# Rotary embedding and attention scores: three of the k loads issued by GpSimd over 15 of the 16 DMA engines

## The chip, the core and the metric

The kernel runs on one core of a Trainium2 chip. TensorE (PE) multiplies matrices into PSUM, VectorE (DVE) and ScalarE (ACT) work on tiles and copy out of PSUM, GpSimd (POOL) and SyncE (SP) issue transfers, and sixteen DMA engines move data between the large memory (DRAM) and the on-chip memory (SBUF). The engines run on their own and wait for each other through semaphores. The metric is the time of one execution in microseconds (us) on the device.

## What is computed

Queries `q` and keys `k` have the shape batch 16, sequence 512, heads 16, dimension 64, all float32. Both are rotated by position (the two halves of the 64 values are mixed by `cos` and `sin`), and then each head's queries are multiplied with all keys of the same batch and head:

```python
q1, q2 = q[..., :half_dim], q[..., half_dim:]
cos_q = cos[None, :, None, :]
sin_q = sin[None, :, None, :]
q_rot = np.concatenate([q1 * cos_q - q2 * sin_q, q1 * sin_q + q2 * cos_q], axis=-1)
...
scores = np.einsum('bshd,bthd->bsht', q_rot, k_rot)
return scores.astype(np.float32)
```

The output has 16 x 512 x 16 x 512 values, 268 MB; the two inputs together are 67 MB.

## The kernel before

**Tiling.** A batch's 512 positions are laid over 128 partitions with four positions (C = 4) in each, so a load of q or k for one batch is one transfer of 128 rows of 16 KB, 2048 KB, and it is contiguous in DRAM. There are 64 steps `i` (16 batches x 4 position classes). In a step the scores of 128 positions with all 512 keys are made for 16 heads: eight pairs `p`, each with two matmuls into one of three PSUM tiles `ps` (L364), which ACT copies into a staging tile `st` (L373). When the eighth pair is copied, SP stores the whole staging tile, 128 rows of 32 KB, 4096 KB (L381). There are three staging tiles, so step i + 3 can only be copied into a tile when the store of step i has landed. The first batch is arranged differently: its inputs arrive in four smaller loads (`load_units`), and its four steps are stored in 16 transfers of 1024 KB.

**Rotation and transposes.** DVE rotates q and k in place in the input tiles, with three operations per position class (`rope`, L290). PE transposes the rotated tile in blocks of 128 (L315), and DVE (for q) or ACT (for k) copies the result from PSUM into `qT` or `kT` (L333). The rotation runs one to two steps ahead for q and about a batch ahead for k: in step i the classes i + 2 of q and i + 5 of k are rotated, and the classes i + 1 of q and i + 4 of k are transposed.

**Loads.** q and k have two input tiles each (`q_sb0`, `q_sb1`, `k_sb0`, `k_sb1`), taken in turn by batch. `load(which, b)` adds one transfer to SP's queue. At the end of step i with i % 4 == 3 the load of k for batch i // 4 + 3 is added (L465), at i % 4 == 2 that of q for batch i // 4 + 2 (L463). So SP's queue is: store, store, load q, store, load k and so on, in this order. SP issues a store when ACT has made the last copy into its tile; a load of k follows at once, since its tile was free by then.

**Order and semaphores.** Every operation is written into a `Plan` with an engine, the keys that it reads and the keys that it writes. `resolve` (L38) derives each operation's waits: a reader waits for the last writer of a key, a writer for the last writer and all readers since. A wait that is implied by another one is dropped. An operation's event is its engine's count, or, for a transfer, 16 more on a semaphore of its own. `emit` writes the operations of SP, ACT, POOL and DVE in order with their waits, and PE's steps as a loop of eight steps per turn. The keys of an input tile are `("in", which, b % 2, c)`, one for each position class; `src_key` (L261) gives the key that the rotation and the transposes use.

POOL has no part in the steady work: it builds the identity matrix for the transposes at the start and is then idle.

Of the kernel before, what the change touches and what calls it, by code (L numbers as in the profile page):

```python
# [7 lines left out]
PE, ACT, DVE, POOL, SP = "PE", "ACT", "DVE", "POOL", "SP"  # L8
# [11 lines left out]
class Plan:  # L20
# [17 lines left out]
    def resolve(self):  # L38
        writer, readers, also = {}, {}, {}
        count = {}  # L40
        known = {e: {} for e in (PE, ACT, DVE, POOL, SP)}
        clock = {}

        def merge(a, b):
            for s, v in b.items():
                a[s] = max(a.get(s, 0), v)

        for op in self.ops:
            need = {}
            for k in op.reads:  # L50
                if k in writer:
                    merge(need, dict([writer[k]]))
            for k in op.writes:
                if k in writer:
                    merge(need, dict([writer[k]]))
                for s, v in readers.get(k, {}).items():
                    merge(need, {s: v})
                if k in also and op.sem is None:
                    merge(need, also.pop(k))
            kn = known[op.engine]  # L60
            need = {s: v for s, v in need.items() if kn.get(s, 0) < v}
            if op.engine == PE:
                need.pop(PE, None)
            for s in list(need):
                others = [t for t in need if t != s]
                if any(clock[t, need[t]].get(s, 0) >= need[s] for t in others):
                    del need[s]
            op.waits = need
            for s, v in need.items():
                merge(kn, clock[s, v])  # L70
                merge(kn, {s: v})
            if op.sem is None:
                s, v = op.engine, count.get(op.engine, 0) + 1
            else:
                s, v = op.sem, count.get(op.sem, 0) + 16
            count[s] = v
            op.event = (s, v)
            clock[s, v] = dict(kn)
            clock[s, v][s] = v
            if op.sem is None and op.engine != PE:  # L80
                clock[s, v][op.engine] = v
            for k in op.reads:
                readers.setdefault(k, {})
                merge(readers[k], {s: v})
            for k in op.writes:
                writer[k] = (s, v)
                readers[k] = {}
            for k in op.also:
                also.setdefault(k, {})
                merge(also[k], {s: v})  # L90
        self.count = count
        self.seen = known

    def emit(self, handles, first, period, turns):

        nc = self.nc
        eng = {PE: nc.tensor, ACT: nc.scalar, DVE: nc.vector, POOL: nc.gpsimd, SP: nc.sync}

        def plain(op):  # L100
            waits = list(op.waits.items())
            for s, v in waits[1:]:
                eng[op.engine].wait_ge(handles[s], v)  # L103
            a, b = op.emit()
            for s, v in waits[:1]:
                a.wait_op(handles[s], v, "sem-ge")
            s, _ = op.event
            b.then_inc(handles[s], 1 if op.sem is None else 16)

        for e in (SP, ACT, POOL, DVE):  # L110
            for op in self.ops:
                if op.engine == e:
                    plain(op)
        for s, v in self.count.items():
            if s not in (PE, ACT, DVE, POOL) and self.seen[SP].get(s, 0) < v:
                nc.sync.wait_ge(handles[s], v)

        pe = [op for op in self.ops if op.engine == PE]
        last = first + period * turns
        for op in pe:  # L120
            if op.step < first:
                plain(op)
        body = [[op for op in pe if (op.step - first) // period == j] for j in range(turns)]
        up = {}
        for s in (ACT, DVE):
            seen = []
            for j in range(2):
                seen.append(sum(1 for op in self.ops if op.engine == s and op.sem is None and op.step < first + period * j))
            up[s] = seen[1] - seen[0]
        n = len(body[0])  # L130
        assert all(len(b) == n for b in body)
        waits = []
        for m in range(n):
            w = {}
            for j in range(turns):
                for s, v in body[j][m].waits.items():
                    w[s] = max(w.get(s, 0), v - j * up[s])
            waits.append(w)
        low, regs, now = {}, {}, {}
        for s in (ACT, DVE):  # L140
            vs = []
            for w in waits:
                if s in w:
                    vs.append(w[s])
            assert vs == sorted(vs) and vs[0] > 0, vs
            low[s] = vs[0]
            regs[s] = nc.tensor.alloc_register("wait_" + s)
            nc.tensor.reg_mov(regs[s], vs[0])
            now[s] = vs[0]
        add = mybir.AluOpType.add  # L150
        with nc.Fori(0, turns, engines=[mybir.EngineType.PE], hint_back_edge=False):
            for m, op in enumerate(body[0]):
                ws = list(waits[m].items())
                for s, v in ws:
                    if v != now[s]:
                        nc.tensor.reg_alu(regs[s], regs[s], v - now[s], add)
                        now[s] = v
                for s, v in ws[1:]:
                    nc.tensor.wait_ge(handles[s], nc.tensor.snap(regs[s]))
                a, b = op.emit()  # L160
                for s, v in ws[:1]:
                    a.wait_op(handles[s], regs[s], "sem-ge")
                b.then_inc(handles[PE], 1)
            for s in (ACT, DVE):
                nc.tensor.reg_alu(regs[s], regs[s], low[s] + up[s] - now[s], add)
        for op in pe:
            if op.step >= last:
                plain(op)
# [3 lines left out]
def kernel(  # L172
# [8 lines left out]
    nc = tc.nc  # L181
    fp32 = mybir.dt.float32
    mult = mybir.AluOpType.mult
    add = mybir.AluOpType.add

    B, S, H, D = q.shape
    HD = D // 2
    P = 128
    C = S // P
# [6 lines left out]
    pool = ctx.enter_context(tc.tile_pool(name="sb", bufs=1))  # L196
    psum = ctx.enter_context(tc.psum_pool(name="ps", bufs=1))

    dram = {
        "q": q.rearrange("b (p c) h d -> b p c h d", c=C),  # L200
        "k": k.rearrange("b (p c) h d -> b p c h d", c=C),
    }
    o_v = out.rearrange("b (p c) h t -> b c p h t", c=C)

    ident = pool.tile([P, P], fp32, name="ident")
    cos_t = pool.tile([P, C, HD], fp32, name="cos_t")
    sin_t = pool.tile([P, C, HD], fp32, name="sin_t")
    ss_t = pool.tile([P, C, 2, HD], fp32, name="ss_t")
    part = pool.tile([P, H * D], fp32, name="part")
    stage = [pool.tile([P, H, S], fp32, name=f"st{n}") for n in range(NST_BUFS)]  # L210
    inb = {w: [pool.tile([P, C, H * D], fp32, name=f"{w}_sb{n}") for n in range(2)] for w in "qk"}
    kTb = [pool.tile([P, HP, S], fp32, name=f"kT{n}") for n in range(2)]
# [6 lines left out]
    plan = Plan(nc)  # L219
# [8 lines left out]
    def dma(engine, e, dst, src, sem, reads=(), writes=(), also=()):  # L228
        plan.add(engine, one(lambda: e.dma_start(dst, src)), reads, writes, sem=sem, also=also)
# [9 lines left out]
    def load_units(which, head, heads):  # L239
# [9 lines left out]
            writes=[("unit", which, u) for u in us], also=[x for u in us for x in unit_keys(which, u)],  # L249
        )  # L250

    def load(which, b):
        if b >= B:
            return
        t = inb[which][b % 2]
        dma(
            SP, nc.sync, t.rearrange("p c (h d) -> p c h d", h=H), dram[which][b], f"in_{which}{b % 2}",
            writes=[("in", which, b % 2, c) for c in range(C)],
        )

    def src_key(which, n):  # L261
        return ("unit", which, n) if n < C else ("in", which, n // C % 2, n % C)

    def src_also(which, n):
        return unit_keys(which, n) if n < C else ()

    def rope(which, n):
# [16 lines left out]
            swapped = bass.AP(part.tensor, part.offset + HD, [part.ap[0], (D, H), (-HD, 2), (1, HD)])  # L284
            adds = [(x4, swapped)]
        xs, xc = x.rearrange(sv, **k2), x.rearrange(sv, **k1)
        key, more = src_key(which, n), src_also(which, n)

        def tt(o, a, b, op, reads, writes):
            plan.add(DVE, one(lambda: nc.vector.tensor_tensor(o, a, b, op=op)), reads, writes, also=more)  # L290

        def products():
            tt(pv, xs, ss, mult, [key, "ss"], ["part"])
            tt(xc, xc, cs, mult, [key, "cos"], [key])

        def sums():
            for y, z in adds:
                tt(y, y, z, add, [key, "part"], [key])

        return [products, sums]  # L300

# [2 lines left out]
    def transposed(which, n, g, engine):  # L304
# [10 lines left out]
            done = [nc.tensor.transpose(bank[:, x, :], srcs[x], ident) for x in range(4)]  # L315
            return done[0], done[-1]

        plan.add(PE, emit, [src_key(which, n), "ident"], [("bank", m)], also=src_also(which, n))
        src = bank
        if which == "q":  # L320
            dst = qTb[n % 2][:, 4 * g : 4 * g + 4, :]
# [180 lines left out]
```

## Time and profile before

| | us |
|---|---|
| median of 3 runs (803.38 to 803.93) | 803.67 |
| the profiled execution | 804.24 |
| its span, first to last instruction | 802.5 |

What the transfers look like, from the list of DMA issues (size and median time from issue to landing):

| transfer | count | KB each | us to landing |
|---|---|---|---|
| store of a staging tile | 60 | 4096 | 24.7 |
| load of k | 15 | 2048 | 27.7 |
| load of q | 15 | 2048 | 28.7 |
| store of a quarter, first batch | 16 | 1024 | 12.3 |

The time to landing includes the wait behind the transfers that were issued earlier. In all, 67.24 MB are read and 268.44 MB written, 418 GB/s over the span. SP waits 722.3 us in total for ACT's copies, which is its normal state: it issues a store when the tile is full. A reader should take the DMA share as the mean over the sixteen engines: a share of 0.06 can be one engine that works while fifteen stand still.

### The profile page before, as it was taken

What the parts mean: (1) busy time and instruction counts of PE and PEld (TensorE: products, weight loads), DVE (VectorE), ACT (ScalarE), POOL (GpSimd) and SP (SyncE); (2) the same over time, 40 slices, a digit from 0 to 9 for tenths busy, and PEclk for the clock granted to TensorE, in tenths of its full rate; (3) what the DMA queues carried; (4) which work ended last, traced back from release to release, by engine and by line L of the source; (5) the groups of instructions that cost most, each with busy time, mean ns of one, the idle gap of its engine ahead of it and who ended that gap; (6) DMA issues with size and microseconds to landing.
All of it is one profiled execution on the core that took longest, in us unless ns stands there. A gap on an engine that the chain in (4) does not pass through costs nothing.

```text
span 802.5 us, 8182 instructions
## 1 busy us (share of the span) xinstructions
PE 688.5 (86%) x3072; PEld 298.0 (37%) x3072; DVE 545.2 (68%) x516; ACT 562.5 (70%) x647; POOL 0.7 (0%) x6
## 2 busy tenths in 40 slices
PE   3989998998979989698896988979879899789970
PEld 2444443333424334243342433434333344334430
DVE  6999987666767668576585866848758477585400
ACT  2978886866858668586676866768757687678770
POOL 0000000000000000000000000000000000000000
PEclk9999999998999989999899999989989799899995
DMA  9999999999999999999999999999999999998994
GB/s 347 419 425 435 432 414 426 427 433 433 426 430 432 427 439 417 441 425 439 428 430 434 431 432 426 437 430 423 426 428 407 433 412 420 429 434 358 419 439 199
DMA packets 17681, 335.87 MB, mean 419 GB/s; under 512 B 1792, under 2 KB 3072, under 8 KB 4096
## 3 DMA queue, kind: packets, MB, share of 16 engines
q1 hardware_dynamic: 17376, 335.55, 98.3%
q10 hardware_dynamic: 288, 0.13, 0.1%
q8 instruction: 6, 0.10, 0.0%
q14 instruction: 11, 0.09, 0.0%
HBM read 67.24 MB, written 268.44 MB: 418 GB/s over the span
## 4 chain that ended last, share of the span: by engine, by line
DMA 48%; PE 38%; DVE 6%; ACT 5%; issue 0%; ACTq 0%; DVEq 0%; SPq 0%
DMA out_dram<-st 47%; PE ps L364 28%; PE bank L315 9%; ACT st L373 5%; DVE part L290 2%; DVE st L290 2%; DVE k_sb L290 1%; DVE q_sb L290 1%; DMA st<-in_k_dram 1%; DVE kT L333 0%; DVE qT L333 0%; ACTq L103 0%; DVEq L103 0%; SPq L497 0%; SPq L468 0%
## 5 line engine op out<-in xcount | busy, mean ns | idle before, releaser
L373 ACT COPY st<-ps 128x1024 f32<-128x1024 f32 x512 | 495.6, 1018 | 203.1 <-DMA out_dram<-st 102.4
L364 PE MATMUL ps<-kT,qT 64*128 64x512 f32 x2048 | 545.8, 649 | 74.7 <-ACT st L373 74.7
L364 PEld LDWEIGHTS ps<-kT,qT 64*128 64x128 f32 x2048 | 183.7, 196 | 265.0 <-issue 137.6
L333 DVE COPY qT<-bank 128x512 f32<-128x512 f32 x118 | 81.5, 691 | 202.8 <-PE bank L315 202.8
L315 PEld LDWEIGHTS bank<-ident,q_sb 128*128 128x128 f32 x480 | 55.6, 152 | 103.0 <-issue 99.5
L315 PE MATMUL bank<-ident,q_sb 128*128 128x128 f32 x480 | 87.0, 309 | 1.0 <-DVE q_sb L290 1.0
L315 PEld LDWEIGHTS bank<-ident,k_sb 128*128 128x128 f32 x480 | 50.5, 141 | 93.4 <-DVE k_sb L290 43.8
L315 PE MATMUL bank<-ident,k_sb 128*128 128x128 f32 x480 | 78.7, 287 | 1.2 <-DVE qT L333 0.8
L333 ACT COPY kT<-bank 128x512 f32<-128x512 f32 x122 | 72.6, 598 | 6.8 <-PE bank L315 6.8
L290 DVE TENSOR_TENSOR part<-q_sb,ss_t 128x1024 f32<-128x1024 f32 x60 | 73.5, 1225 | 3.0
L290 DVE TENSOR_TENSOR q_sb<-q_sb,cos_t 128x1024 f32<-128x1024 f32 x60 | 73.5, 1225 | 2.1
L290 DVE TENSOR_TENSOR k_sb<-k_sb,cos_t 128x1024 f32<-128x1024 f32 x60 | 73.5, 1225 | 2.0
L290 DVE TENSOR_TENSOR k_sb<-k_sb,part 128x1024 f32<-128x1024 f32 x60 | 73.5, 1225 | 2.1
L290 DVE TENSOR_TENSOR part<-k_sb,ss_t 128x1024 f32<-128x1024 f32 x60 | 72.9, 1215 | 0.3
L290 DVE TENSOR_TENSOR q_sb<-q_sb,part 128x1024 f32<-128x1024 f32 x60 | 72.9, 1215 | 0.0
L315 PE MATMUL bank<-ident,st 128*128 128x128 f32 x64 | 10.7, 318 | 13.3 <-DVE st L290 13.3
L315 PEld LDWEIGHTS bank<-ident,st 128*128 128x128 f32 x64 | 8.3, 161 | 18.5 <-DVE st L290 16.8
L290 DVE TENSOR_TENSOR part<-st,ss_t 128x1024 f32<-128x1024 f32 x8 | 9.8, 1223 | 6.4 <-DMA st<-in_k_dram 6.1
L290 DVE TENSOR_TENSOR st<-st,part 128x512 f32<-128x512 f32 x16 | 11.1, 691 | 0.5
L290 DVE TENSOR_TENSOR st<-st,cos_t 128x1024 f32<-128x1024 f32 x8 | 9.8, 1225 | 0.3
L333 ACT COPY qT<-bank 128x512 f32<-128x512 f32 x10 | 5.7, 617 | 3.5 <-PE bank L315 3.5
L333 DVE COPY kT<-bank 128x512 f32<-128x512 f32 x6 | 4.1, 684 | 0.1
(9 smaller groups left out, 2.8 us busy)
## 6 DMA issues: line engine op xcount, KB each, us to landing
out_dram<-st SPq DMA_DIRECT2D x60, 4096.0 KB, 24.7
k_sb<-in_k_dram SPq DMA_DIRECT2D x15, 2048.0 KB, 27.7
q_sb<-in_q_dram SPq DMA_DIRECT2D x15, 2048.0 KB, 28.7
out_dram<-st SPq DMA_DIRECT2D x16, 1024.0 KB, 12.3
st<-in_k_dram SPq DMA_DIRECT2D x1, 1536.0 KB, 9.1
st<-in_q_dram SPq DMA_DIRECT2D x1, 1536.0 KB, 12.4
st<-in_k_dram SPq DMA_DIRECT2D x1, 512.0 KB, 5.1
st<-in_q_dram SPq DMA_DIRECT2D x1, 512.0 KB, 5.7
```

Source lines behind the costliest of these rows:

```text
L290: plan.add(DVE, one(lambda: nc.vector.tensor_tensor(o, a, b, op=op)), reads, writes, also=more)
L315: done = [nc.tensor.transpose(bank[:, x, :], srcs[x], ident) for x in range(4)]
L333: plan.add(engine, one(lambda: copy(out=dst, in_=src)), [("bank", m)], keys)
L364: nc.tensor.matmul(out=ps[:, r, :], lhsT=lhs[lo:hi, :], rhs=rhs[lo:hi, :], start=True, stop=True)
L373: plan.add(ACT, one(lambda: nc.scalar.copy(out=so, in_=si)), [("ps", y)], [("st", s, p)])
```

## The change

Three loads, those of k for the batches 5, 9 and 13, are no longer one transfer of 128 rows in SP's queue. GpSimd loads rows 0 to 119, and SP loads the last eight rows at the old place in its queue. Ahead of its load GpSimd issues two small things: an instruction with the mode `reset_dge_cursor`, and a load of five rows of four values into a new tile `scratch`. [...] Each of the 120 rows is written as two pieces of 8 KB, the second half first.

```diff
+    RELIEVED = {("k", 5): 0, ("k", 9): 1, ("k", 13): 2}
+    SLOW = 4
     def load(which, b):
...
         t = inb[which][b % 2]
-        dma(
-            SP, nc.sync, t.rearrange("p c (h d) -> p c h d", h=H), dram[which][b], f"in_{which}{b % 2}",
-            writes=[("in", which, b % 2, c) for c in range(C)],
-        )
+        sem = f"in_{which}{b % 2}"
+        rows = [("in", which, b % 2, c) for c in range(C)]
+        rest = [("in rest", which, b % 2, c) for c in range(C)]
+        if (which, b) not in RELIEVED:
+            dma(SP, nc.sync, t.rearrange("p c (h d) -> p c h d", h=H), dram[which][b], sem, writes=rows + rest)
+            return
+        n, E, F = 120, C * H * D, C * H * D // 2
+        x = RELIEVED[which, b]
+        plan.add(POOL, None, (), rows)
+        src = bass.AP(q.tensor, 512 * x, [(512, SLOW + 1), (64, 2), (1, 2)])
+        dst = scratch[: SLOW + 1, 4 * x : 4 * x + 4].rearrange("p (a b) -> p a b", a=2)
+        dma(POOL, nc.gpsimd, dst, src, "cursor", writes=[("scratch", x)])
+        d = dram[which][b]
+        src = bass.AP(d.tensor, d.offset + F, [(E, n), (-F, 2), (1, F)])
+        dst = bass.AP(t.tensor, t.offset + F, [(t.ap[0][0], n), (-F, 2), (1, F)])
+        dma(POOL, nc.gpsimd, dst, src, f"part{x}", writes=rows)
+        dma(SP, nc.sync, t[n:].rearrange("p c (h d) -> p c h d", h=H), d[n:], sem, writes=rest)
```

The operation with `None` in place of an instruction is where GpSimd waits until PE has read the tile's former contents and then resets the cursor; `resolve` gives it waits but no event:

```diff
+            if op.emit is None:
+                for s, v in waits:
+                    eng[op.engine].wait_ge(handles[s], v)
+                nc.gpsimd.inc_swdge_sem([], [], mode="reset_dge_cursor")
+                return
```

The two parts of a load have keys and semaphores of their own, so whoever reads an input tile now reads both keys: `src_key` becomes `src_keys` with `"in"` and `"in rest"`. In the built program this adds one semaphore to the wait of the first DVE operation on each relieved tile, and SP's final wait gets the scratch loads' semaphore. Apart from that the instructions of PE, ACT, DVE and SP stand in the same order as before; the three SP loads have eight rows instead of 128.

More of the change, by code (lines that the diff above doesn't have):

```diff
@@ L71, in resolve @@
                 merge(kn, {s: v})
+            if op.emit is None:
+                continue
             if op.sem is None:
@@ L101, in plain @@
             waits = list(op.waits.items())
+            if op.emit is None:
+                for s, v in waits:
+                    eng[op.engine].wait_ge(handles[s], v)
+                nc.gpsimd.inc_swdge_sem([], [], mode="reset_dge_cursor")
+                return
             for s, v in waits[1:]:
@@ L209 @@
     part = pool.tile([P, H * D], fp32, name="part")
+    scratch = pool.tile([P, 128], fp32, name="scratch")
     stage = [pool.tile([P, H, S], fp32, name=f"st{n}") for n in range(NST_BUFS)]
@@ L255, in load, with src_keys @@
         t = inb[which][b % 2]
-        dma(
-            SP, nc.sync, t.rearrange("p c (h d) -> p c h d", h=H), dram[which][b], f"in_{which}{b % 2}",
-            writes=[("in", which, b % 2, c) for c in range(C)],
-        )
-    def src_key(which, n):
-        return ("unit", which, n) if n < C else ("in", which, n // C % 2, n % C)
+        sem = f"in_{which}{b % 2}"
[15 more added lines that the diff above has]
+        dma(SP, nc.sync, t[n:].rearrange("p c (h d) -> p c h d", h=H), d[n:], sem, writes=rest)
+    def src_keys(which, n):
+        if n < C:
+            return [("unit", which, n)]
+        return [(name, which, n // C % 2, n % C) for name in ("in", "in rest")]
     def src_also(which, n):
@@ L286, in rope @@
         xs, xc = x.rearrange(sv, **k2), x.rearrange(sv, **k1)
-        key, more = src_key(which, n), src_also(which, n)
+        keys, more = src_keys(which, n), src_also(which, n)
         def tt(o, a, b, op, reads, writes):
@@ L292, in products @@
         def products():
-            tt(pv, xs, ss, mult, [key, "ss"], ["part"])
-            tt(xc, xc, cs, mult, [key, "cos"], [key])
+            tt(pv, xs, ss, mult, keys + ["ss"], ["part"])
+            tt(xc, xc, cs, mult, keys + ["cos"], keys)
         def sums():
             for y, z in adds:
-                tt(y, y, z, add, [key, "part"], [key])
+                tt(y, y, z, add, keys + ["part"], keys)
         return [products, sums]
@@ L316, in emit @@
             return done[0], done[-1]
-        plan.add(PE, emit, [src_key(which, n), "ident"], [("bank", m)], also=src_also(which, n))
+        plan.add(PE, emit, src_keys(which, n) + ["ident"], [("bank", m)], also=src_also(which, n))
         src = bank
```

## The prediction

> **What bounds the kernel now.** I read the page first: busy shares, the 40 slices, the DMA queues.
>
> ```profile
> span 802.5 us, 8182 instructions
> PE 688.5 (86%) x3072; PEld 298.0 (37%) x3072; DVE 545.2 (68%) x516; ACT 562.5 (70%) x647; POOL 0.7 (0%) x6
> ...
> DMA  9999999999999999999999999999999999998994
> GB/s 347 419 425 435 432 414 426 427 433 433 426 430 432 427 439 417 441 425 439 428 430 434 431 432 426 437 430 423 426 428 407 433 412 420 429 434 358 419 439 199
> ...
> q1 hardware_dynamic: 17376, 335.55, 98.3%
> ```
>
> No compute engine is the limit: PE is busy 86%, DVE and ACT about 70%. The DMA engines are busy in every slice, and the one queue in use takes 98.3% of sixteen engines' span. Only two places show less: a dip near the 37th slice (358 GB/s) and the last slice (199 GB/s). So I asked for the busy time by stretches (each row: start:end, length, the five engines with their instruction counts, PE clock, DMA share, GB/s).
>
> ```profile
> 350.00:550.00 200.00, 176.28 (x778) 75.44 (x778) 137.22 (x129) 140.80 (x161) 0.00 (x0) 0.93 1.00 431
> ...
> 728.00:732.00 4.00, 4.00 (x21) 1.80 (x20) 3.90 (x4) 3.76 (x6) 0.00 (x0) 1.00 0.25 107
> 732.00:734.00 2.00, 2.00 (x12) 0.91 (x10) 1.29 (x3) 1.82 (x2) 0.00 (x0) 1.00 0.65 279
> ...
> 790.00:792.00 2.00, 0.00 (x0) 0.00 (x0) 0.00 (x0) 0.00 (x0) 0.00 (x0) 0.50 0.65 279
> 792.00:794.00 2.00, 0.00 (x0) 0.00 (x0) 0.00 (x0) 0.00 (x0) 0.00 (x0) 0.50 0.11 49
> 794.00:799.80 5.80, 0.00 (x0) 0.00 (x0) 0.00 (x0) 0.00 (x0) 0.00 (x0) 0.50 0.05 23
> ```
>
> In the middle sixteen engines together move 431 GB/s, 26.9 each. In the last 8 us they move 49 and then 23 GB/s: a share of 0.05 is about one engine of sixteen. The DMA view of 792 to 800 us, in slices of 0.2 us, shows what that is:
>
> ```profile
> DMA  3030000003000003000003000003000003000000
> GB/s 164 0 164 0 0 0 0 0 0 164 0 0 0 0 0 164 0 0 0 0 0 164 0 0 0 0 0 164 0 0 0 0 0 164 0 0 0 0 0 0
> DMA packets 10, 0.23 MB, mean 29 GB/s; under 512 B 3, under 2 KB 3, under 8 KB 3
> ```
>
> One packet of 164 x 0.2 = 33 KB begins every six slices, 1.2 us: from the tenth slice on a single engine finishes its rows alone. At 1.00 share in 744 to 790 us the rest had no idle time to spare, so this engine was behind. The packet records say why: between 300 and 308 us one chain of 32 KB store packets takes 1246 to 1265 ns each, the others 1213. Of the sixteen completion increments of a store, the last came 4.8 us after the first near 220 us, 9.0 near 413 and 12.4 near 729, while the second-last was 4.7, 5.2 and 3.4 behind. One engine falls about 0.3 us behind per store (8 packets x 40 ns), the other lags do not grow.
>
> The lag has two costs. At the end thirteen engines stop near 791.7 (the 790 to 792 row) and the slow one at 799.9: 8.2 us. And at 728 to 734 us the others wait for it, 4 x 0.75 + 2 x 0.35 = 3.7 us on average: by the chain of waits
>
> ```profile
> 697.58 23.82 DMA out_dram<-st
> 722.54 2.08 PE ps L364 x4
> ```
>
> a stage tile is free at 721.4, when the slow engine has stored its part; only then do ACT and PE go on, and the next store is issued at 732. Without that wait the slow engine would be 8.2 + 3.7 = 11.9 us behind the bulk.
>
> **The change part by part.** *Relief.* A load of k is 2048 KB, 128 KB or eight 16 KB rows for each engine: 128 / 26.9 = 4.87 us. In three loads the engine left out gets none of the 120 rows. SP's eight rows are unshown as a shape. At one end none falls on it (relief 3 x 4.87 = 14.6 us), at the other all eight (0). Wide transfers here spread evenly, so I take one row on each of eight engines, it among them: 7/8 x 14.6 = 12.8 us. The slow engine then ends at 799.9 - 12.8 = 787.1. The three loads were issued at 151.9, 349.3 and 548.1 us, when it was about 4, 7 and 12 us behind the first engine, so relief of 4.3 each time is not wasted in idling ahead.
>
> *The others.* Their bulk ended at 791.7 and waited 3.7: 788.0 without the wait. Eight of them get one row more per load, 3 x 0.61 = 1.8 us: 789.8. The last of them trails. In 792 to 794 us the share 0.11 is 0.11 x 2 x 16 = 3.5 engine-us, 2.0 of the slow one and 1.5 of another, so the second-last ended about 2.0 after the bulk; bounds 0 (lags come and go) and the 3.4 seen at 729. I take 2.0: 791.8.
>
> *Price of a load in GpSimd's queue.* Not shown before. Its rows are cut into two 8 KB pieces. The nearest rows are the 8 KB store rows of the first 16 stores: 20 to 64 us ran at 423 GB/s, 1.9% below 431, 0.1 us of a 4.87 us load, 0.3 in three. The dear end comes from the worst load packets of the trace: between 110 and 114 us eleven of 16 KB took 0.92 to 1.73 us, 1.29 in the mean, where 0.61 is usual. If all rows of the relieved loads were that slow, each load would take about twice its 4.87 us. So the bounds are 0 and 4.87 a load. I take 0.3: 792.1.
>
> [...]
>
> *Instructions moved and added.* SP loses no instruction: each relieved load still issues, with eight rows (0.94 us at 151.89, next store 10 us later at 162.06). POOL, with 0.7 us of work, gets per load a wait on PE, the cursor instruction, a tiny load into scratch and the 120 rows; nothing is queued behind them but the next load. Cost nothing: they start when PE's last transposes of that buffer end, 149.4 us at the first, 2.5 us before SP's turn. DVE gets one more semaphore to wait for, once per relieved load, four steps (about 38 us) after issue, while k landed after 27.7 us (median). Were that cover gone, DVE would hold both the rotation and the qT copies that PE needs, and each us late would be one on the path.
>
> *Overtaking.* The 120 rows no longer stand behind stores in SP's queue, so up to two stores may land up to 4.87 us later, and the stage tile with them. That load landed 23.9 us after issue; the store issued at 162.06 came behind it, at 175.8, 13.7 us of cover. 4.87 later leaves 8.9, more than any lag left. I cost it at 0. In the tail PE needs 10.0 us a step against 9.7 for a store (707.6, 717.6, then 732, 742): when the wait at 722 is gone up to 1.5 us of compute may show.
>
> *Sum.* Last engine 792.1 instead of 799.9: -7.8. The profiled execution took 804.24 (span 802.5 and 1.7 around it), the median of the three is 803.67; I take the gain off the median: **795.9 us**. Its own range: -11.6 (neither spread nor extra rows, end 788.3) to -4 (spread 3.4, compute 1.5, a load's price 0.5 each), 792 to 799.7.
>
> **The rivals.**
> *A, the slow engine is not the one left out.* The trace names no engine, so that it is number 4, or that the scratch load really sets the next transfer past it, is read nowhere. Then its 24 rows stay, and SP's spread rows may add three: 0 to +1.8 us on the engine that ends last, 803.7 to **805.5**, slower. For it: the number is nowhere in the profile. Against: one engine and no other is steadily slow, and the rows removed (12.8 us) are close to its lag (11.9). It decides as soon as fewer than a row is taken off it.
> [...]
>
> *B, the GpSimd load costs what the relief brings.* All fifteen engines carry it, so its price lies on the new path in full. At 2.6 us a load (7.8 / 3) nothing is left; at half a doubling, 2.4 each, **803.2**; at the full one 810. For it: nothing like it in the trace. Against: the engines take packets of one queue with 3 ns gaps, and q10's two loads at the start did no visible harm.
>
> *C, overtaking stalls the stages.* One 4.87 us stall that nothing hides: **800.8**. Against: the cover above.
>
> **How the numbers follow.** Forecast 0.54, A 0.22, B 0.20, C 0.04. A measurement here tells about 0.2%, 1.6 us, from no change. Faster: 0.54 + 0.04 + 0.06 of B = 0.64. Same: 0.05 of A and 0.05 of B = 0.10. Slower: 0.17 of A and 0.09 of B = 0.26. Range: from 792.0, the forecast's good end, to 805.5, A's end; left out about 0.04 below, 0.11 above (B's dear half and the worst of A).
>
> **What would show it.** Right: no single-engine tail of 8 us; the last share below 1.00 lasts 2 to 4 us; no 0.25 stretch near 728; stores issued at about 10 us steps there; three GpSimd transfers of some 1920 KB in a queue of their own. A: the tail of one engine stays 8 to 10 us. B: GB/s drops below 420 around 150, 350 and 550 us. C: DMA share falls below 1.00 some 10 to 20 us after those times. The prediction is wrong if the tail goes and the time doesn't follow, or if a second engine takes the slow one's place.

## The result and the profile after

The change made no difference: 804.83 us (median of 4 runs, 804.15 to 805.27) against 803.80 for the kernel before in the same session, a ratio of 1.0011 with a 95% interval of 0.9994 to 1.0029. The forecast was 795.9, 1% faster. Two large things happened and cancelled.

The page of the changed kernel: span, rate in 40 slices, and the two queues that carry loads and stores.

```profile
span 803.3 us, 8192 instructions
...
GB/s 342 425 423 426 433 425 433 401 370 430 434 433 426 439 429 431 433 381 374 434 429 432 430 432 436 428 437 368 401 423 433 431 433 435 432 435 429 434 432 295
...
q1 hardware_dynamic: 16992, 329.65, 97.0%
q0 software_dynamic: 912, 5.90, 2.3%
```

The dip of before near the 37th slice (358) is gone and the last slice holds 295 instead of 199. But there are three new dips, in the slices 8 and 9, 18 and 19, 28 and 29, just where the three GpSimd loads run. The stretches show both (start:end, length, five engines, PE clock, DMA share, GB/s):

```profile
156.00:168.00 12.00, 12.00 (x58) 5.18 (x58) 10.45 (x11) 10.09 (x12) 0.00 (x0) 1.00 1.02 299
355.00:368.00 13.00, 13.00 (x64) 5.58 (x61) 11.46 (x11) 11.22 (x14) 0.00 (x0) 1.00 1.03 283
554.00:568.00 14.00, 14.00 (x70) 6.26 (x68) 12.02 (x11) 12.31 (x15) 0.00 (x0) 1.00 1.02 300
728.00:732.00 4.00, 4.00 (x22) 1.93 (x22) 3.90 (x4) 3.77 (x6) 0.00 (x0) 1.00 0.97 418
...
794.00:800.20 6.20, 0.00 (x0) 0.00 (x0) 0.00 (x0) 0.00 (x0) 0.00 (x0) 0.50 0.49 211
```

The three places of the dips in the kernel before:

```profile
156.00:168.00 12.00, 12.00 (x59) 5.19 (x56) 10.49 (x11) 10.09 (x13) 0.00 (x0) 1.00 1.02 434
355.00:368.00 13.00, 13.00 (x66) 6.07 (x66) 11.36 (x12) 11.58 (x15) 0.00 (x0) 1.00 1.02 437
554.00:568.00 14.00, 14.00 (x70) 6.38 (x71) 12.35 (x12) 12.43 (x16) 0.00 (x0) 1.00 1.01 419
```

Read the two last columns together. The DMA share is 1.00 or more in both kernels, so no engine stood idle, and yet the rate fell from 434 to 299 GB/s: the packets themselves took longer. Against 434, 437 and 419 GB/s the three dips lose 12 x 135/434 + 13 x 154/437 + 14 x 119/419 = 3.7 + 4.6 + 4.0 = 12.3 us of transfer. On the other side, 728 to 732 us runs at 0.97 instead of 0.25, and from 794 us on the share is 0.49 instead of 0.05: the single-engine tail is gone. By the last store's sixteen completion increments, the engines ended before at 791.9 to 793.8 and one at 800.3; now they end between 794.3 and 801.0, the second-last only 0.5 before the last.

The list of transfers shows one more thing (size, median us from issue to landing):

```profile
k_sb<-in_k_dram POOLq DMA_DIRECT2D x3, 1920.0 KB, 29.8
```

A GpSimd load does not overtake. It has its own queue, but lands 29.8 us after issue, about as late as through SP's queue (27.7). In the packet records its 240 pieces, 16 on an engine, alternate one by one with SP's packets.

The same records give the first lead. Mean packet times in microseconds, from the traces:

```
kernel, stretch in us          stores 32 KB   SP loads 16 KB   GpSimd pieces 8 KB
before, 156 to 166             1.22           0.62             -
after,  158 to 166             -              1.01             0.49
after,  172 to 178             1.21           -                0.31
```

Beside stores a GpSimd piece takes the usual 0.31 us. Beside the load of q that SP issued a little earlier, it and the q packets take some 60% longer. The engine that GpSimd leaves out is no exception. It can be followed by the 4-byte packets of GpSimd's queue that it takes one by one between SP's rows, and its own eight q rows beside the three loads took 8.3, 8.8 and 8.3 us instead of 8 x 0.61 = 4.9.

### The profile page after: what moved, and what is told of

Its sections match the earlier page's. It is cut to its first block, busy times and chain, and to the rows that moved or that the text cites. A ratio compares the mean times of both kernels' runs of the same rounds, so it can differ in the third digit from the quotient of the medians.

```text
span 803.3 us, 8192 instructions
## 1 busy us (share of the span) xinstructions
PE 680.6 (85%) x3072; PEld 295.1 (37%) x3072; DVE 544.8 (68%) x516; ACT 562.1 (70%) x647; POOL 4.8 (1%) x12
## 4 chain that ended last, share of the span: by engine, by line
DMA 48%; PE 35%; DVE 8%; ACT 5%; issue 1%; ACTq 0%; DVEq 0%; SPq 0%
DMA out_dram<-st 47%; PE ps L393 27%; PE bank L344 9%; ACT st L402 5%; DVE st L319 3%; DVE part L319 2%; DVE k_sb L319 2%; DVE q_sb L319 1%; DMA st<-in_k_dram 1%; DVE kT L362 0%; DVE qT L362 0%; ACTq L110 0%; DVEq L110 0%; SPq L526 0%; SPq L497 0%
## 5 line engine op out<-in xcount | busy, mean ns | idle before, releaser
L393 PE MATMUL ps<-kT,qT 64*128 64x512 f32 x2048 | 539.1, 643 | 81.8 <-ACT st L402 81.7
L393 PEld LDWEIGHTS ps<-kT,qT 64*128 64x128 f32 x2048 | 181.7, 194 | 268.7 <-issue 135.1
L237 POOL DMA_DIRECT2D scratch<-in_q_dram x3 | 1.8, 616 | 543.2 <-PE bank L344 543.2
## 6 DMA issues: line engine op xcount, KB each, us to landing
k_sb<-in_k_dram POOLq DMA_DIRECT2D x3, 1920.0 KB, 29.8
```

The costliest lines, as they stand in the source:

```text
L393: nc.tensor.matmul(out=ps[:, r, :], lhsT=lhs[lo:hi, :], rhs=rhs[lo:hi, :], start=True, stop=True)
```

## The experiments

Theories, formed on this: (1) two streams of load packets obstruct each other; (2) the 120 rows are dealt to the engines by neighbouring eights, and engines then meet where the rows are written; (3) any GpSimd load costs the engines some time; (4) the pieces of 8 KB in reversed order cost it. Where the slow engine is concerned, the rival was that another engine than the one left out is slow.

**e1_late: GpSimd waits for the load of q.**

```diff
-        plan.add(POOL, None, (), rows)
+        plan.add(POOL, None, [("in", "q", (b - 1) % 2, 0)], rows)
```

> The changed kernel with one more wait: GpSimd starts each of its three loads only when the load of q that SP issued just before has landed. Theory 1 (two streams of load packets that alternate on the same engines obstruct each other, the dip at 157 to 169 us is the q load beside the GpSimd load): the 8 KB pieces take 309 ns as they did beside stores, the three dips of 4 to 5 us each go, and with the slow engine relieved the time falls to 791 to 796 us. Theory 2 (eight neighbouring rows to one engine clash at the memory's write side): the same here, since the clash needs a second writer. Rival theory 3 (any GpSimd load costs the engines some 4 us, by its descriptors): the dips move to the new place and the time stays near 804.

Measured: 799.3 us, ratio 0.9942 (0.9921 to 0.9963): 0.6% faster than before, and less than expected (791 to 796). The stretches of this run, the first the place of the old dip, the second the new place of the load (issued at 166.4), the others the tail:

```profile
156.00:168.00 12.00, 12.00 (x60) 5.26 (x58) 10.49 (x11) 10.23 (x12) 1.43 (x2) 1.00 1.01 431
166.00:194.00 28.00, 23.97 (x108) 9.93 (x106) 17.17 (x17) 18.77 (x22) 1.19 (x2) 0.94 1.01 421
728.00:732.00 4.00, 4.00 (x22) 1.83 (x20) 3.29 (x4) 3.82 (x5) 0.00 (x0) 1.00 0.95 410
...
790.00:794.80 4.80, 0.00 (x0) 0.00 (x0) 0.00 (x0) 0.00 (x0) 0.00 (x0) 0.50 0.05 20
```

The dip is gone, 431 GB/s, and the new place loses only 28 x 10/431 = 0.6 us against 431; pieces there take 0.31 us once the last load packets of SP are through. Theory 3, with its 4 us a load, falls. Theories 1 and 2 both expected the dip to go. But a tail of one engine is back: a share of 0.05, from 791.0 to 795.3 us.

**e2_late_slow9: the same with `SLOW = 9`.** The edit on top of e1_late:

```diff
-    SLOW = 4
+    SLOW = 9
```

> As e1_late, with the constant SLOW set to 9, so that engine 9 is the one left out and the scratch load has ten rows. If the slow engine is number 4 and the scratch load sets the next transfer as its source says, one engine again ends 8 us or more after the rest, with a DMA share near 0.05 there, and the time is 803 to 806. If the gain of e1_late came from anything else than relieving engine 4, the time stays at that of e1_late.

Measured: 809.14 us, ratio 1.0057 (1.0038 to 1.0077). Its tail:

```profile
734.00:740.00 6.00, 6.00 (x31) 2.71 (x30) 4.30 (x5) 5.57 (x7) 0.00 (x0) 1.00 0.33 142
...
800.60:806.10 5.50, 0.00 (x0) 0.00 (x0) 0.00 (x0) 0.00 (x0) 0.00 (x0) 0.50 0.06 24
```

The wait for one engine (0.33 at 734 to 740 us) and the lone tail are both there again, longer than expected. One constant, and with it ten rows in the scratch load instead of five, makes 9.8 us of difference to e1_late, so leaving out the engine that the constant 4 stands for is what relieves the slow one. The packets agree: the engine left out, followed by its 4-byte packets, takes 1.23 to 1.28 us for a store with the constant 4 (570 to 579 us in e1) and 1.213 with the constant 9 (372 to 378 us here).

**e3_pool128: whole loads by GpSimd, early.**

```diff
-        n, E, F = 120, C * H * D, C * H * D // 2
...
-        dma(POOL, nc.gpsimd, dst, src, f"part{x}", writes=rows)
-        dma(SP, nc.sync, t[n:].rearrange("p c (h d) -> p c h d", h=H), d[n:], sem, writes=rest)
+        dma(POOL, nc.gpsimd, t.rearrange("p c (h d) -> p c h d", h=H), dram[which][b], f"part{x}", writes=rows + rest)
```

> The three loads go by GpSimd at the same early time as in the changed kernel, but whole: all 128 rows on all sixteen engines, no scratch load, no cursor, no eight rows by SP, rows in one piece of 16 KB. The slow engine gets no relief. Theory 1 (two load streams at once obstruct each other): the dips near 157 to 169, 356 to 368 and 556 to 568 us stay, load packets of q take about 1.0 us instead of 0.61, and the time is 810 to 817. Theory 2 (the 120 rows dealt by eights clash at the memory's write side): no dips, load packets at 0.61, time 803 to 805.

Measured: 805.57 us, ratio 1.0016 (1.0002 to 1.0031), just above the 803 to 805 of theory 2. There is no dip where the load runs beside the load of q:

```profile
154.00:166.00 12.00, 12.00 (x58) 5.12 (x56) 10.35 (x10) 10.04 (x12) 0.00 (x0) 1.00 0.99 426
```

Between 156 and 166 us 104 load packets of SP and 124 of GpSimd all take 0.61 us. Theory 1 falls: in this run two load streams share the engines without loss, and the transfer has 128 rows.

**e4_pool128_halves: the same with reversed 8 KB pieces.** The three-dimensional pattern of the changed kernel with n = 128, no scratch load, no rows by SP.

> As e3_pool128 (128 rows by GpSimd, early, beside the load of q), but each row written as two pieces of 8 KB, the second half first, as in the changed kernel. Theory 2 (rows dealt to the engines by neighbouring eights clash where they are written): no dip if 128 rows are still dealt as in e3_pool128, 8 KB pieces at 309 ns, time 803 to 806. Theory 4 (the 8 KB pieces in reversed order cost the time): the dips of 4 to 5 us return, pieces at 460 to 500 ns, time 812 to 818. If the three-dimensional pattern makes GpSimd deal 128 rows by neighbouring eights too, theory 2 also expects the dips, and e5 and e7 must tell.

Measured: 806.78 us in one run, beside 804.75 of before. The time is a little above the expected 803 to 806, but 178 pieces beside the load of q take 0.31 us, the q packets 0.62. Theory 4 falls.

**e5_pool120_whole: 120 rows in one piece each.**

```diff
-        src = bass.AP(d.tensor, d.offset + F, [(E, n), (-F, 2), (1, F)])
-        dst = bass.AP(t.tensor, t.offset + F, [(t.ap[0][0], n), (-F, 2), (1, F)])
+        src = bass.AP(d.tensor, d.offset, [(E, n), (1, E)])
+        dst = bass.AP(t.tensor, t.offset, [(t.ap[0][0], n), (1, E)])
```

> The changed kernel with the 120 rows in one piece of 16 KB each. Theory 2 (dealt by eights): the dips stay, q load packets at about 1.0 us and GpSimd's 16 KB pieces about as slow, time as the changed kernel or, if the pattern without pieces goes to other engines and the slow one keeps its rows, 812 to 818. Theory 4 (reversed 8 KB pieces): no dips, all load packets at 0.61 us, time 791 to 806 according to whether the slow engine is left out.

Measured: 822.69 us in one run. From 160 to 170 us SP's load packets take 1.20 us and GpSimd's 1.17 instead of 0.61. The stretch:

```profile
156.00:176.00 20.00, 20.00 (x98) 8.83 (x97) 14.64 (x14) 16.33 (x19) 0.00 (x0) 1.00 1.02 281
```

So it is the 120 rows, not the reversed pieces. The time is above what either theory gave. Part of that can be read: the engine left out, followed again by its 4-byte packets, takes 1.213 us for a store (165.9 to 169.6 us), so it is not the slow one, which kept its rows; one engine ended 5.1 us after the second-last. How much each part costs was not measured.

**e7_sp120: the 120 rows by SP, no GpSimd at all.**

```diff
-        dma(POOL, nc.gpsimd, dst, src, f"part{x}", writes=rows)
+        dma(SP, nc.sync, t[:n].rearrange("p c (h d) -> p c h d", h=H), d[:n], f"part{x}", writes=rows)
```

> No GpSimd: SP loads rows 0 to 119 in one transfer and the last eight in another, both at the old place in its queue, 16 KB pieces. 120 rows are 15 shares of eight; the slow engine may or may not be among the fifteen. Theory 2 (rows dealt by neighbouring eights clash at the written side): the packets of these three loads take about 1.0 to 1.2 us instead of 0.61 with no second queue and no GpSimd in play, and each load loses 3 to 5 us. Theory 4 (8 KB pieces) and any theory that blames GpSimd's queue: 0.61 us, no dip, time 803 to 806.

Measured: 811.48 us in one run, 6.7 above the median of before (804.75). Within one kernel the load of q, 128 rows, takes 0.61 us a packet (158 to 162 us), and the 120 rows behind it 1.17 (172 to 180). The stretch with the 120 rows:

```profile
169.00:181.00 12.00, 9.63 (x40) 4.08 (x38) 7.14 (x8) 6.75 (x8) 0.00 (x0) 0.86 1.03 304
```

The doubling needs neither GpSimd nor its queue.

**e10_sp_halves: SP loads rows 0 to 63, then 64 to 127.** As e7_sp120 with `n = 64`. It asks whether the number fifteen matters or that neighbouring rows are taken together.

> No GpSimd, all sixteen engines, no odd number of shares: SP loads each of the three tiles as rows 0 to 63 and then rows 64 to 127, at the old place in its queue. [...] Rival (what cost time in e7_sp120 and the changed kernel is the split over fifteen engines as such): packets at 0.61 us and the time of before, 803 to 807.

Measured: 809.64 us in one run, beside 804.33 of before. That is 5.3 us more, above the 803 to 807 of the rival and well below the 14.6 us that three fully doubled loads would add (3 x 4.87, the author's estimate). The packets are doubled all the same: 102 load packets between 172 and 180 us take 1.22 us, twice 0.61 (in the second and third load 1.17 and 1.14, at 372 to 376 and 572 to 576 us):

```profile
170.00:180.00 10.00, 7.57 (x30) 3.04 (x30) 4.49 (x6) 5.66 (x7) 0.00 (x0) 0.83 1.01 256
```

The number fifteen is not needed. Together with e3, e4 and e7 this shows that the price belongs to the rows that one transfer takes: with 120 or 64 neighbouring rows and other loads at work the packets take about twice as long (1.17 us in e7, 1.14 to 1.22 in e10), with all 128 they take 0.61 (e3) and 0.62 (e4). That this is so because of how the rows are dealt to the engines is argued: no trace shows which rows an engine takes. Nor do the runs separate the two ends of a transfer, since another deal changes the addresses read in DRAM as well as the partitions written; that the engines meet where the rows are written stays the author's guess.

**e9_early_slow9: the price without the relief.** The changed kernel with `SLOW = 9`:

```diff
-    SLOW = 4
+    SLOW = 9
```

> The changed kernel as it was (GpSimd early, beside the load of q) with SLOW = 9: all of the price and none of the relief. If the changed kernel came out even because three early loads cost about 13 us and the relief brought about 12, the dips stay and the time is 813 to 820, with one engine alone at the end. If the early loads were cheap and the relief small, it is 804 to 808.

Measured: 814.19 us, ratio 1.0101 (1.0066 to 1.0136). Dip and lone tail stand in one run:

```profile
155.00:167.00 12.00, 12.00 (x60) 5.34 (x58) 9.84 (x11) 10.48 (x12) 0.00 (x0) 1.00 0.97 307
...
804.60:810.10 5.50, 0.00 (x0) 0.00 (x0) 0.00 (x0) 0.00 (x0) 0.00 (x0) 0.50 0.06 24
```

Four kernels now form a table of ratios to the kernel before, each with its 95% interval and each against the kernel before in its own session:

```
                          SLOW = 4 (relief)               SLOW = 9 (no relief)
GpSimd early (beside q)   1.0011 (0.9994 to 1.0029)       1.0101 (1.0066 to 1.0136)
GpSimd late (after q)     0.9942 (0.9921 to 0.9963)       1.0057 (1.0038 to 1.0077)
```

Down a column, the place of the load is worth 0.7% and 0.4%, 3.5 to 5.5 us; along a row, the relief is worth 0.9% and 1.2%, 7 to 9 us. The 0.4% is not certain, since its two intervals overlap; the other three differences are clear. The changed kernel is the corner where price and relief cancel.

**e6_late_four and e8_late_five: more relief.** Both stand on top of e1_late. There one engine again ended last, so a fourth load was relieved, then five were.

```diff
-    RELIEVED = {("k", 5): 0, ("k", 9): 1, ("k", 13): 2}
+    RELIEVED = {("k", 5): 0, ("k", 9): 1, ("k", 13): 2, ("k", 15): 3}
...
+    RELIEVED = {("k", 4): 0, ("k", 7): 1, ("k", 10): 2, ("k", 13): 3, ("k", 15): 4}
```

> As e1_late (GpSimd waits for the load of q), with a fourth relieved load, k of batch 15. In e1_late one engine again ended 4.3 us after the second-last and 9.5 after the first. If that is the slow engine, 4.3 us more relief puts it level with the second-last: 795 to 796.5. If it is another engine, nothing is gained and a fourth load's price is paid: 799 to 801.

Measured: 798.48 us, ratio 0.9911 (0.9882 to 0.9940), between the two ranges. Its interval overlaps that of e1_late (0.9921 to 0.9963), so it decides neither way.

> As e6_late_four, with five relieved loads, k of the batches 4, 7, 10, 13 and 15. In e6_late_four one engine still ended 2.8 us after the second-last and 7.5 after the first. If the slow engine still sets the end and a relief is worth about 2.5 us to it and costs the rest about 1.2, the time falls by 1 to 2 us more, to 795.5 to 797.5. If the price of a load has caught up with the relief, it stays at 798 to 800.

Measured: 796.96 us, ratio 0.9890 (0.9858 to 0.9922), the lowest median of the study and faster than both kernels it started from. The gap between last and second-last engine shrinks from 4.3 us (three loads) over 2.8 to 0.7 (five), in the profiled execution of each. It does so mostly because the second-last ends later, at 791.0, 792.4 and 794.1 us, while the last ends at 795.3, 795.1 and 794.9. In e8 the last one's store packets take 1.213 us from 708 us on, so it is not the slow engine any more. e6 and e8 overlap within their intervals; a sixth load would probably have little left to gain, which was not tried.

## Why the prediction was wrong

**The step that failed is "Price of a load in GpSimd's queue".** It took 0.1 us a load, 0.3 for three, from the 8 KB store rows as the nearest. By the rate in the dips the three loads cost 3.7, 4.6 and 4.0 us, 12.3 in all; by the ends of the engines, which set the time, some 8: in e9 the slow engine ended at 810.2 us instead of 800.3, and 1.8 of these 9.9 us are SP's three extra rows. The row was near in piece size, and piece size alone cost nothing (e4); what mattered was that a transfer takes 120 rows, and no row of before had a load of other than 128 rows to compare. Its dear bound, 4.87 us a load from eleven slow load packets, supposed a doubling, and e7 and e10 measured one, 1.17 and 1.22 us for 0.61; that the eleven packets have the same cause is not shown. The slowing was measured with other loads at the same time, a second load in the changed kernel (1.01 and 0.49 us) or the same load on the other engines in e7 and e10; beside stores (e1) the pieces ran at 0.31.

**The same step charged only the fifteen engines, and that failed too.** The prediction put the relieved engine at 787.1 us, free of any price. In the changed kernel its last packet ended at 798.1, where it had ended at 799.9. Its q rows beside the three loads took 3.4, 3.9 and 3.4 us longer than usual, 10.7 in all, which nearly uses up the 12.8 us of rows taken off it.

**Rival B was the case that came true**, at 803.2 and a chance of 0.20. Its sign, GB/s below 420 near 150, 350 and 550 us, is the one that the trace after shows. Its "for" (nothing like it in the trace) was a stronger argument than it was given: an operation that no row shows, with 14.6 us between its bounds against a gain of 7.8, deserved more than a fifth. The prediction's own sign of being wrong came as well: the tail goes, the time doesn't follow, and a second engine takes the slow one's place (the last one's store packets take 1.213 us from 650 us on).

**Bound and relief: right in kind, the second too large.** One slow engine sets the end of the kernel before; with SLOW = 4 it is the one left out (rival A falls: e2 and e9 bring its tail back). The packet chain of that engine in e1, followed through the third load, carries no GpSimd piece and a single 16 KB row of SP's eight, so seven of eight rows were taken off, as assumed. But from 12.8 us of rows the slow engine gained only 800.3 - 795.3 = 5.0 in e1, where no load of q runs beside the pieces. About 4.1 of the difference can be a price that the late loads still have: in e2, where it keeps its 24 rows and gets SP's three, it ended at 806.2, 5.9 later than before, 1.8 by rows and 4.1 otherwise. In e1 four of its store packets, at 580 to 586 us while other engines took GpSimd's pieces, lasted 1.46 to 1.50 us instead of 1.24; the engine left out in e2 shows the same (1.41 to 1.64 at 381 to 390 us). The remaining 3.7 us were not settled. The other engines ended at 785.8 to 791.0 in e1; the step "the others" had 791.8.

**The wait in the tail: right.** With the lag smaller the stretch at 728 to 732 us runs at 0.97 (0.95 in e1) and the next stores follow. Relief is not the only way to this: in e10, without any, it runs at 0.99; there the other engines end 4 to 6 us later than before.

**Overtaking: wrong in its premise, right in its cost.** The load did not land earlier (29.8 us after issue); the two queues alternate packet by packet. Rival C's stall never came: the DMA share is 1.00 through the dips and after.

**The balance.** By the packet records, packet time beyond the usual 1.213, 0.611 and 0.309 us adds up to 7.8 us an engine before and 16.7 after. The engines other than the last ended at 792.1 on average before, 3.7 of it waiting, and at 797.7 after: 9.3 us more work, 0.9 of it the rows taken from the slow engine and the rest the slower packets. So they arrive where the slow one used to, the last at 801.0, and the time stands still.

**Smaller slips.** The good end of the prediction's own range holds; its other end adds up to -3.7 us, not -4 (1.4 of spread, 1.5 of compute and 1.2 of price off 7.8). Rival B's 803.2 counts the 0.3 of the forecast's price twice. Its "3 ns gaps" between packets are overlaps: in the records a packet starts 3 to 4 ns before the end of the one ahead. None of this changes the reading.

## What to carry to other kernels

When fifteen of sixteen DMA engines are idle at the end, look for one engine with slow packets and take rows off it; here that is worth about 1% (e8, ratio 0.9890). But here a transfer of 120 or 64 rows instead of 128 doubled the time of its packets (1.17 to 1.22 us for 0.61, e7 and e10) and of those of the load beside it (1.20, e5), and even the engine that took none of its rows slowed (8.3 to 8.8 us for 4.9, the changed kernel), at a DMA share of 1.01 to 1.03: read GB/s, not the share (299 for 434 in the first dip), and try such a transfer beside stores, where its pieces took the usual 0.31 us (e1). Where a change rests on an operation that no row of the trace shows, measure it alone first.

## What the runs showed of the hardware

- One engine's 32 KB store packets take 1.244 us in the mean where the others' take 1.213, in every run looked at; its loads are not slower (0.613). Its slow packets end with PE's work: in the kernel before the last ends at 779.3 us, PE's last matmul at 778.7 (774.2 and 773.5 in e1, 783.9 and 783.0 in e2), and from then on it takes 1.213 too. What slows it is not shown. By e1 against e2 (799.3 and 809.14 us) it is the engine that the constant 4 leaves out; no trace names it.
- Two loads of 64 rows took up to twice the packet time of one of 128 (1.14 to 1.22 us in e10 against 0.61), from SP's queue; the packets of loads of 120 rows took 1.17 us from SP's queue (e7) and from GpSimd's (e5).
- In the changed kernel and e1 two queues share an engine packet by packet: a row of 32 KB (1.213 us), a piece of 8 KB (0.31 us), and so on. The engine that GpSimd leaves out takes 4-byte packets of that queue instead, about as many as another engine takes pieces (16 a load), 9 to 18 ns each. By them it can be picked out in the packet records.
